# A retention layer's q and k of two heads as one seven-product block, three weight sums on GpSimd, and Newton's step with scalars

## The chip, the cores and the metric

The kernel runs on one core of a Trainium2 chip. The metric is the device time of one execution in microseconds (us), the median of several runs. One execution was also taken with the hardware profiler; all rows quoted come from such an execution. The engines are TensorE (PE; its weight loads are PEld), VectorE (DVE), ScalarE (ACT), GpSimd (POOL) and SyncE (SP, which here only issues transfers).

## The reference

A trunk of two layers over 512 tokens of 1024 channels, in float32. What matters here is the token half of a layer:

```python
proj = x @ w_in[i]
q_na, k_na, v_na, q_r, k_r, v_r, g_r, gate_a, gate_b = jnp.split(proj, IN_SPLITS, axis=-1)
ya = neighbourhood_attention(q_na, k_na, v_na, na_rpb[i])
yb = bidirectional_retention(q_r, k_r, v_r, g_r, ret_decay_f[i], ret_decay_b[i])
merged = sigmoid(gate_a) * (ya @ w_branch_a[i]) + sigmoid(gate_b) * (yb @ w_branch_b[i])
x = layer_norm(ALPHA * x + merged @ w_out[i], ln1_g[i], ln1_b[i])
ffn = conv_glu_ffn(x, w_up[i], conv_w[i], conv_b[i], w_down[i])
x = layer_norm(ALPHA * x + ffn + ple, ln2_g[i], ln2_b[i])
```

Retention has four heads; q_r and k_r have 128 channels per head, v_r and g_r 256. q_r and k_r are turned by a rotary embedding (cosine and sine of the position, the two halves of the 128 channels exchanged) and k_r is scaled by 128 ** -0.5. Each head then works in chunks of 128 tokens, forwards and backwards, with decays that are exponentials of learnt rates times distances.

## The kernel before

**Precision.** PE multiplies in a rounded form of float32. Every operand is therefore split into a high part (the rounded value, made by ACT) and a low part (the rest, a subtraction on DVE); `split` does this, and `mm3` issues three matmuls for one product: high by high, high by low, low by high.

**Weights.** All weights are packed as chunks of 128x1024 (512 KB), `wpack[l, c]`. A `Stream` holds the list of all chunks in the order of use. `load` issues transfers from SP into staging buffers (a ring of three, `raw`, or a buffer of the unit pool, `rawa` and `rawt` in the traces), `prep` splits a chunk into high and low parts (in a ring of three pairs, or in units where the chunk is "held"), and `get` hands it over and prepares some that follow.

**Blocks of seven products.** A projection can be cut into 2x2 blocks of inputs and outputs and done by seven block products instead of eight (Strassen's scheme in Winograd's form). The products are called `a`, `c`, `t1`, `t2`, `d`, `t3`, `t4`. The sums of weights that they need are made by transfers that add: `Stream.add` issues from POOL a transfer that reads a second chunk and adds it to the staging buffer. An `Item` is one chunk of this list; `plus` names the chunk to be added, `nxt` the item that takes over its staging buffer. The sums of the activations (`Sx`) are made once for each layer in `vg_sums`. Values and gates of retention are two such blocks (0 and 1, with outputs along the free dimension), and three blocks of gate columns (2, 3, 4) are done transposed by `gate_block` and `product_t`: 256 output columns by 512 tokens, in 24 matmuls of 128x256 for each product. Each block ends in `gate_out`, a sigmoid and a transfer to memory.

**Heads of q and k.** `q_head` and `k_head` do one head in a plain product: `gemm_t`, 24 matmuls of 128x512, then `rotated` (three multiplications by cosine and sine on DVE, an addition, a split). `q_head` also makes the head's decays (`decays`: two DVE operations and three exponentials on ACT) and a second q scaled by them (`qx`).

**Order.** After the values and gates of a layer comes the filling stretch. `FILL` is its list of pieces, written out by hand: products of blocks 2 to 4 (`2a` ... `4t4`), heads (`q0`, `k0`, ...), queries, keys and values of the attention (`nq`, `nk`, `vn`), and projections of the branches (`bb`). `RET_AT` and `NA_AT` say at which place of the list each head of retention and attention starts; its steps are put between the pieces. `ret_head` is a generator: scores and kz transposes first (`s`, `kz`), then the state (`st`), the output (`o`), the transposes (`ybt`). In this stretch a scheduler orders the instructions of each engine from the order of the program and the data; each engine then carries out its own list strictly in order, with semaphores between. In the other stretches the order is kept as written.

**The end.** The last layer norm of the last tile (tile 3) is done by `last_tile`: ACT's square root, then `refine` (a reciprocal and one step of Newton's method on values of one column), then two halves scaled and sent. Tile 2 is finished before by `norm_b`, whose last step is an addition on POOL and a transfer from SP.

Of the kernel before, what the change touches and what calls it, by code (L numbers as in the profile page):

```python
# [10 lines left out]
F32R = mybir.dt.float32r  # L11
# [4 lines left out]
P = 128  # L16
# [23 lines left out]
DEEP = 5  # L40

XN_AT = (0, 0, 0, 0)

FILL = ('2a', '3a', '2c', '3c', 'q0', '2t1', '3t1', 'k0', '2t2', '3t2', '2d', '3d', '4a', '2t3', '3t3', '4c', '2t4', '4t1', 'k1', '3t4', '4t2', '4d', 'q1', '4t3', '4t4', 'nk0', 'nq0', 'k2', 'q2', 'nk1', 'q3', 'nq3', 'k3', 'nq1', 'nk2', 'nq2', 'nk3', 'vn', 'bb0', 'bb1', 'bb2', 'bb4', 'bb5', 'bb6', 'bb7', 'xn', 'bb3')
# [22 lines left out]
VG_EARLY = "d"  # L67
VG_HELD = (('0t1', '1t1', '0t2', '0c', '1t2', '1a', '1d', '1t3'), ('0a', '0c', '0t1', '1t1', '1t3', '1t2', '0t3', '0t2', '1d'))

# [47 lines left out]
def trunk(tc, wpack, x_nat, x_tr, head, p_tr, rpb, decay, ln_par, ln_col, conv, cos_t, sin_t, dist, xi_d, zd, mask, ident_d, out):  # L117
# [4 lines left out]
    with ExitStack() as es:  # L122
# [50 lines left out]
        class Item:  # L173
# [7 lines left out]
            def __init__(self, kind, src, width, pool=None, plus=None, own=None):  # L181
                self.kind, self.src, self.width, self.pool, self.plus, self.own = kind, src, width, pool, plus, own
                self.raw = self.hl = None
                self.nxt = self.early = self.block = None
                self.sent = kind == "w" and any(a <= src[1] < b for a, b in SENT)

        def block_items(pos, held, early, n=2):
# [44 lines left out]
        def fill_items(l):  # L232
            by = {}

            for b in range(2, 5):
                pos = {(q, 0): (l, (36, 40, 56)[b - 2] + i, 0, 1024) for i, q in enumerate("acbd")}
                for it in block_items(pos, {}, VG_EARLY, 1):
                    by[f"{b}{it.kind}"] = [it]
# [36 lines left out]
        class Stream:  # L275
# [59 lines left out]
            def prep(self, n, part=None):  # L335
                while self.nprep < min(n, len(self.seq)):
# [317 lines left out]
        for l in range(DEPTH):  # L654
# [133 lines left out]
            def rotated(t1, ps, sc):  # L788
# [13 lines left out]
                return u  # L802

            def decays(h):

# [9 lines left out]

            kfs = {}

            def gate_a(m):
# [4 lines left out]
            def q_head(h):  # L823
                wx[h] = decays(h)
                t1 = tmp("t1")
                qr[h] = rotated(t1, gemm_t(xs), None)
                nc.vector.tensor_mul(t1, t1, wx[h][:, 1, :])
                u = qx[h] = unit_r("qx")
                split(u[:, 0, :], u[:, 1, :], t1)

            def k_head(h):
# [3 lines left out]
                kr[h] = rotated(kf[h], gemm_t(xs), P ** -0.5)  # L835


            def ret_head(h):
                q, k, k1, W = qr.pop(h), kr.pop(h), kf.pop(h), wx.pop(h)[:, 0, :]
                A = []  # L840
                for c in range(2):
# [3 lines left out]
                    for i in range(2):  # L845
                        m = slice((2 * c + 1 - i) * P, (2 * c + 2 - i) * P)
                        mm3(ps[:, i * 256:(i + 1) * 256], k[:, 0, m], k[:, 1, m], q[:, 0, n], q[:, 1, n], True, True)
                    ta = tmp("ta")
# [29 lines left out]
                for tq in range(2):  # L878
                    ps = bank("o")
                    for i in range(2):  # L880
# [7 lines left out]
                        d = slice((1 - tq) * 256, (2 - tq) * 256)  # L888
                        mm3(o, qq[:, 0, c], qq[:, 1, c], su[:, 0, d], su[:, 1, d], False, True)
                    st = sp.tile([P, 2, 6], F32, tag="bn", name=nm("gn"))  # L890
# [204 lines left out]
            def gate_block(b, kind):  # L1095
# [34 lines left out]
                else:  # L1130
                    assert (b, "p5") not in keep
                    product_t(kind, u[b], False)
                    t = tmp("sgb")
                    nc.scalar.activation(t, u[b], AF.Sigmoid)
# [31 lines left out]
            def fillers():  # L1166
                for i, f in enumerate(FILL):
# [3 lines left out]
                    if f == "xn":  # L1171
                        plain_x()
                        continue
                    if f[0] in "234":
                        gate_block(int(f[0]), f[1:])
# [242 lines left out]
            for s, n in enumerate(SEGS):  # L1418
# [254 lines left out]
def _pack(w_in, w_ba, w_bb, w_out, w_up, w_down, w_pg, w_pp):  # L1673
# [3 lines left out]
    for hp in range(2):  # L1677
        ch += list(vr[hp]) + list(gr[hp])
        for h in (2 * hp, 2 * hp + 1):
            ch += [qr[h], kr[h]]  # L1680
# [88 lines left out]
```

## Time and profile before

| | us |
|---|---|
| median of 3 runs | 1684.12 (1683.38 to 1684.5) |
| the profiled execution, its own time | 1682.4 |
| its span, first to last instruction | 1680.6 |

The granted clock of TensorE was 0.998 in this execution. A row of a group gives the line, the engine, the operation, out<-in with shapes, the number of instructions, their busy time and the mean duration of one in ns, and the idle time of the engine just before them. A row in order of time gives start and duration in us. A line number is often that of a helper; names of tiles tell more. "lo<-raw" is the DVE half of a split of weights, "hi<-raw" the ACT half.

### The profile page before, as it was taken

How to read it: one execution, taken by the hardware profiler on the slowest of the kernel's cores; microseconds unless marked ns; L12 is line 12 of the kernel's file. 1: busy time of each engine (PE TensorE's matmuls, PEld its weight loads, DVE VectorE, ACT ScalarE, POOL GpSimd, SP SyncE). 2: the span in 40 equal slices, each digit the busy share in tenths (PEclk: the TensorE clock that was granted, in tenths of full speed). 3: DMA queues.
4: the chain of work that ended last, by engine and by line, in shares of the span. 5: the costliest groups of instructions: out<-in, count | busy, mean ns of one | idle time of the engine just before them, and what ended most of it. 6: DMA issues, size and time to landing. Idle time of an engine off the chain costs nothing.

```text
span 1680.6 us, 22093 instructions
## 1 busy us (share of the span) xinstructions
PE 1668.9 (99%) x8327; PEld 1417.6 (84%) x8327; DVE 1229.6 (73%) x1860; ACT 951.7 (57%) x1420; POOL 187.8 (11%) x213
## 2 busy tenths in 40 slices
PE   9999999999999999999999999999999999999997
PEld 7889988888888888888888899888888888888886
DVE  7656677776788767767876567777698887676678
ACT  6764676863366545344476647768534574453454
POOL 1111111100200100000112011111002010000003
PEclk9999999999999999999999999999999999999999
DMA  8989666666655535535779796666667464264274
GB/s 305 251 229 240 166 147 138 170 168 233 200 131 168 121 113 160 139 103 177 200 225 220 183 246 158 139 141 168 169 242 236 129 167 121 88 198 115 89 213 100
DMA packets 87530, 290.20 MB, mean 173 GB/s; under 512 B 9984, under 2 KB 14592, under 8 KB 87424
## 3 DMA queue, kind: packets, MB, share of 16 engines
q1 hardware_dynamic: 62368, 199.66, 33.4%
q0 software_dynamic: 25056, 89.14, 29.7%
q8 instruction: 65, 1.06, 0.3%
q14 instruction: 41, 0.34, 0.1%
HBM read 269.89 MB, written 17.83 MB: 171 GB/s over the span
## 4 chain that ended last, share of the span: by engine, by line
PE 98%; DVE 1%; ACT 0%; issue 0%; DVEq 0%; ACTq 0%
PE gt L90 31%; PE u L90 13%; PE v L90 7%; PE gt L397 6%; PE gt L398 6%; PE gt L399 6%; PE w L90 4%; PE gn L398 3%; PE gn L399 3%; PE gn L397 3%; PE x L90 1%; PE u L397 1%; PE u L399 1%; PE u L398 1%; PE gn L90 1%; PE na L1023 1%
## 5 line engine op out<-in xcount | busy, mean ns | idle before, releaser
L90 PE MATMUL gt<-x1t,hi 128*128 128x512 f32 x1408 | 433.4, 389 | 0.0
L90 PEld LDWEIGHTS gt<-x1t,hi 128*128 128x128 f32 x1408 | 264.3, 188 | 54.6
L90 PE MATMUL gt<-x1t,lo 128*128 128x512 f32 x704 | 274.1, 389 | 0.1
L90 DVE TENSOR_TENSOR lo<-raw,hi 128x1024 fp32r<-128x1024 f32 (+1 forms) x147 | 176.0, 1207 | 44.1 <-ACT hi L90 44.0
L90 DVE SCALAR_TENSOR_TENSOR ca<-gt,cw,ca 128x511 f32<-128x511 f32 x176 | 131.8, 749 | 78.2 <-ACT ca L90 75.1
L90 ACT CAST hi<-raw 128x1024 fp32r<-128x1024 f32 (+1 forms) x147 | 151.3, 1039 | 34.2 <-PE u L90 15.1
L90 PEld LDWEIGHTS gt<-x1t,lo 128*128 128x128 f32 x704 | 132.1, 188 | 28.6 <-DVE lo L90 1.0
L90 DVE TENSOR_TENSOR lo<-rawa,hi 128x1024 fp32r<-128x1024 f32 x94 | 109.8, 1177 | 48.8 <-ACT hi L90 48.6
L90 ACT ACTIVATE ca<-gt,cw 128x512 f32<-128x512 f32 x88 | 68.7, 780 | 131.3 <-PE gt L90 131.3
L90 ACT CAST hi<-rawa 128x1024 fp32r<-128x1024 f32 x94 | 94.5, 1016 | 39.0 <-DMA rawa<-in_wpack 14.1
L90 POOL DMA_DIRECT2D rawa<-in_wpack x72 | 65.1, 949 | 367.9 <-DVE lo L90 315.1
L397 PE MATMUL gt<-xt,hi 128*128 128x512 f32 x256 | 100.8, 394 | 0.0
L398 PE MATMUL gt<-xt,hi 128*128 128x512 f32 x256 | 99.8, 390 | 0.0
L399 PE MATMUL gt<-xt,lo 128*128 128x512 f32 x256 | 99.7, 389 | 0.0
L170 ACT CAST hi<-raw 128x1024 fp32r<-128x1024 f32 x44 | 45.9, 1053 | 75.1 <-issue 29.6
L355 ACT CAST hi<-raw 128x1024 fp32r<-128x1024 f32 x48 | 50.5, 1053 | 48.8 <-PE gt L398 41.1
L357 POOL DMA_DIRECT2D lo<-in_wpack x48 | 42.2, 879 | 294.3 <-ACT lo L356 221.1
L90 POOL DMA_DIRECT2D rawt<-in_wpack x20 | 18.8, 1007 | 380.5 <-DMA rawt<-in_wpack 371.9
L171 DVE TENSOR_TENSOR lo<-raw,hi 128x1024 fp32r<-128x1024 f32 x44 | 53.4, 1224 | 10.7 <-ACT hi L170 10.2
L399 PEld LDWEIGHTS gt<-xt,lo 128*128 128x128 f32 x256 | 48.1, 188 | 10.3
L90 PE MATMUL v<-hi,sa 128*128 128x512 f32 x176 | 56.2, 389 | 0.0
L397 PEld LDWEIGHTS gt<-xt,hi 128*128 128x128 f32 x256 | 48.2, 188 | 9.1
(353 smaller groups left out, 4219.6 us busy)
## 6 DMA issues: line engine op xcount, KB each, us to landing
raw<-in_wpack SPq DMA_DIRECT2D x235, 512.0 KB, 3.6
rawa<-in_wpack POOLq DMA_DIRECT2D x84, 512.0 KB, 6.4
lo<-in_wpack POOLq DMA_DIRECT2D x48, 512.0 KB, 5.4
rawa<-in_wpack SPq DMA_DIRECT2D x28, 512.0 KB, 6.8
rawt<-in_wpack SPq DMA_DIRECT2D x28, 512.0 KB, 6.7
rawt<-in_wpack POOLq DMA_DIRECT2D x28, 512.0 KB, 7.6
r_scr<-pp SPq DMA_DIRECT2D x8, 512.0 KB, 10.1
gb<-gb_scr SPq DMA_DIRECT2D x8, 512.0 KB, 4.8
```

The source lines that it names most:

```text
L90: r = f(*a, **k)
L170: nc.scalar.copy(hi, src)
L171: nc.vector.tensor_sub(lo, src, _f(hi))
L355: nc.scalar.copy(hi[:, cs], it.raw[:, cs])
L357: nc.gpsimd.dma_start(lo[:, cs], wpack[l, c][:, o:o + w], accum_op=ALU.add)
L397: nc.tensor.matmul(ps, lh, rh, start=start, stop=False, skip_group_check=more)
L398: nc.tensor.matmul(ps, lh, rl, start=False, stop=False, skip_group_check=more)
L399: nc.tensor.matmul(ps, ll, rh, start=False, stop=stop, skip_group_check=more)
L1023: nc.tensor.matmul(ov[kt], lv, pt[kt // 2][:, sp_, c], start=i == 0 and sp_ == 0, stop=i == 3 and sp_ == 1)
```

## The change

Three edits, with the orders that belong to them.

1. q and k of retention heads 0 and 1 become block 5 of the filling stretch: a transposed block of seven products over the 256 columns of q and the 256 of k together. `gate_block` and `product_t` do it as they do blocks 2 to 4; in place of the sigmoid and the transfer, `qk_out` does rotary embedding, scaling and splits for one half of the tokens and q or k of both heads at a time. Q, QX and K then lie in two tiles for two halves of the tokens, and `ret_head` reads them through small functions (`whole`, `halves`). The four pieces `q0`, `k0`, `q1`, `k1` leave `FILL`, seven pieces `5a` to `5t4` enter it and the others are put in a new order; `RET_AT` and `NA_AT` are moved by three. The decays of both heads are made at the first half of q.
2. `POOLED`: for `t2` and `t3` of block 2 and `t2` of block 3 the chunk `d` is not added by a transfer, but by an addition on POOL from the staging buffer of item `d`, after that item has been split.
3. In `refine` the product of the variance with the reciprocal twice is a `tensor_scalar` with two per-partition scalars instead of a `scalar_tensor_tensor`.

In layer 0 product `t2` of block 1 is no longer held in units.

```diff
+POOLED = ('t2 t3', 't2', '', '')
...
-FILL = ('2a', '3a', '2c', '3c', 'q0', '2t1', '3t1', 'k0', '2t2', '3t2', '2d', '3d', '4a', '2t3', '3t3', '4c', '2t4', '4t1', 'k1', '3t4', '4t2', '4d', 'q1', '4t3', '4t4', 'nk0', 'nq0', 'k2', 'q2', 'nk1', ...)
-RET_AT = (21, 26, 30, 34)
-NA_AT = (36, 36, 39, 40, 42, 43, 43, 44)
+FILL = ('2a', '3a', '2c', '3c', '2t1', '3t1', '2d', '3d', '2t2', '3t2', '5a', '5c', '4a', '5t1', '2t3', '3t3', '2t4', '5t2', '5d', '3t4', '4c', '5t3', '4t1', '5t4', '4d', '4t2', '4t3', 'k2', '4t4', 'q2', 'nk0', 'nq0', 'nk1', ...)
+RET_AT = (24, 29, 33, 37)
+NA_AT = (39, 39, 42, 43, 45, 46, 46, 47)
...
-VG_HELD = (('0t1', '1t1', '0t2', '0c', '1t2', '1a', '1d', '1t3'), ...)
+VG_HELD = (('0t1', '1t1', '0t2', '0c', '1a', '1d', '1t3'), ...)
...
-                    it = Item(kind, at(src), pos["a", j][3], plus=at(plus), own=kind in ("a", "t3"), pool=held.get(kind))
+                    it = Item(kind, at(src), pos["a", j][3], plus=None if kind in pooled.split() else at(plus), own=kind in ("a", "t3"), pool=held.get(kind))
...
+            for it in out:
+                if it.kind in pooled.split():
+                    [o for o in out if o.kind == "d"][0].into.append(it)
...
-                        else:
+                        elif it.nxt.plus is not None:
                             self.add(it.nxt)
+                    for o in it.into:
+                        nc.gpsimd.tensor_add(o.raw, o.raw, it.raw)
...
+            def qk_out(fh, th, src):
+
+                v = lambda t: t.rearrange("p (h n) -> p h n", h=2)
+                n = slice(th * 256, (th + 1) * 256)
+                trig = lambda t, p: _ap(t[p], th * 256, [[0, 2], [1, 256]])
+                if fh == 0:
+                    t1 = v(tmp("t1"))
+                else:
+                    if 0 not in kfs:
+                        kfs[0] = unit_f("kf", (P, 2, 512))
+                    t1 = kfs[0][:, :, n]
+                t2 = tmp("t2")
+                lo, hi, al = slice(0, 64), slice(64, 128), slice(0, 128)
+                for o, i, tb in ((t1, al, cos_sb), (v(t2[hi]), lo, sin_sb), (v(t2[lo]), hi, sin_sb)):
+                    if fh == 0:
+                        nc.vector.tensor_mul(o, v(src[i]), trig(tb, i))
+                    else:
+                        nc.vector.scalar_tensor_tensor(o, v(src[i]), -P ** -0.5, trig(tb, i), op0=ALU.mult, op1=ALU.mult)
+                nc.vector.tensor_add(t1, t1, v(t2))
+                d = Qh if fh == 0 else Kh
+                u = d[th] = up.tile([P, 2, 2, 256], F32R, tag="u", name=nm("qk"))
+                split(u[:, 0], u[:, 1], t1)
+                if fh == 0:
+                    for h in range(2):
+                        if h not in wx:
+                            wx[h] = decays(h)
+                        nc.vector.tensor_mul(t1[:, h], t1[:, h], wx[h][:, 1, n])
+                    u = QXh[th] = up.tile([P, 2, 2, 256], F32R, tag="u", name=nm("qx"))
+                    split(u[:, 0], u[:, 1], t1)
...
             def gate_out(b, fh, th, src, scale=1.0):
+                if b == 5:
+                    qk_out(fh, th, src)
+                    return
                 nc.scalar.activation(src, src, AF.Sigmoid, scale=scale)
...
-                    nc.vector.scalar_tensor_tensor(a, r, ve[0], r, op0=ALU.mult, op1=ALU.mult)
+                    nc.vector.tensor_scalar(a, ve[0], r, r, op0=ALU.mult, op1=ALU.mult)
```

More of the change, by code (lines that the diff above doesn't have):

```diff
@@ L67 @@
 VG_EARLY = "d"
-VG_HELD = (('0t1', '1t1', '0t2', '0c', '1t2', '1a', '1d', '1t3'), ('0a', '0c', '0t1', '1t1', '1t3', '1t2', '0t3', '0t2', '1d'))
+VG_HELD = (('0t1', '1t1', '0t2', '0c', '1a', '1d', '1t3'), ('0a', '0c', '0t1', '1t1', '1t3', '1t2', '0t3', '0t2', '1d'))
 def _ap(t, off, dims):
@@ L184, in __init__, with block_items @@
                 self.nxt = self.early = self.block = None
+                self.into = []
                 self.sent = kind == "w" and any(a <= src[1] < b for a, b in SENT)
-        def block_items(pos, held, early, n=2):
+        def block_items(pos, held, early, n=2, pooled=""):
             out = []
@@ L233, in fill_items @@
             by = {}
-            for b in range(2, 5):
-                pos = {(q, 0): (l, (36, 40, 56)[b - 2] + i, 0, 1024) for i, q in enumerate("acbd")}
-                for it in block_items(pos, {}, VG_EARLY, 1):
+            for b in range(2, 6):
+                pos = {(q, 0): (l, (36, 40, 56, 8)[b - 2] + i, 0, 1024) for i, q in enumerate("acbd")}
+                for it in block_items(pos, {}, VG_EARLY, 1, POOLED[b - 2]):
                     by[f"{b}{it.kind}"] = [it]
@@ L802, in rotated @@
                 return u
+            kfs = {}
+            whole = lambda u: lambda s, c: u[:, s, c]
+            Qh, QXh, Kh = {}, {}, {}
+            halves = lambda u, h: lambda s, c: u[c.start // 256][:, s, h, c.start % 256:c.start % 256 + c.stop - c.start]
+            def qk_out(fh, th, src):
[26 more added lines that the diff above has]
+                    split(u[:, 0], u[:, 1], t1)
+                for h in range(2):
+                    if th in d and 1 - th in d:
+                        if fh:
+                            kr[h], kf[h] = halves(Kh, h), kfs[0][:, h]
+                        else:
+                            qr[h], qx[h] = halves(Qh, h), halves(QXh, h)
             def decays(h):
@@ L814, in decays @@
                 return w
-            kfs = {}
             def gate_a(m):
@@ L825, in q_head @@
                 t1 = tmp("t1")
-                qr[h] = rotated(t1, gemm_t(xs), None)
+                qr[h] = whole(rotated(t1, gemm_t(xs), None))
                 nc.vector.tensor_mul(t1, t1, wx[h][:, 1, :])
-                u = qx[h] = unit_r("qx")
+                u = unit_r("qx")
                 split(u[:, 0, :], u[:, 1, :], t1)
+                qx[h] = whole(u)
             def k_head(h):
@@ L834, in k_head @@
                 kf[h] = kfs[h // 2][:, h % 2, :]
-                kr[h] = rotated(kf[h], gemm_t(xs), P ** -0.5)
+                kr[h] = whole(rotated(kf[h], gemm_t(xs), P ** -0.5))
             def ret_head(h):
@@ L1132, in gate_block @@
                     product_t(kind, u[b], False)
+                    if b == 5:
+                        qk_out(0, 1, u[b])
+                        return
                     t = tmp("sgb")
@@ L1173, in fillers @@
                         continue
-                    if f[0] in "234":
+                    if f[0] in "2345":
                         gate_block(int(f[0]), f[1:])
@@ L1678, in _pack @@
         ch += list(vr[hp]) + list(gr[hp])
+        if hp == 0:
+            qk = np.concatenate([q_r[:, :256], k_r[:, :256]], axis=1)
+            ch += [qk.reshape(2, 4, P, 2, 256)[int(k in "cd"), :, :, int(k in "bd")].transpose(1, 0, 2).reshape(P, 1024) for k in "acbd"]
+            continue
         for h in (2 * hp, 2 * hp + 1):
```

6 lines of the change are left out of this document (3 added, 3 removed).

## The prediction

> **What bounds the kernel now.** I read the page first (span, busy time, chain that ended last), then who TensorE (PE) waited for, then PE in order of time where the change lies.
>
> ```profile
> span 1680.6 us, 22093 instructions
> PE 1668.9 (99%) x8327; PEld 1417.6 (84%) x8327; DVE 1229.6 (73%) x1860; ACT 951.7 (57%) x1420; POOL 187.8 (11%) x213
> ...
> PE 98%; DVE 1%; ACT 0%; issue 0%; DVEq 0%; ACTq 0%
> ```
>
> ```profile
> PE warm L504 <- DVE warm L501: 1.2, 1, 1.2
> ```
>
> PE is busy 99% of the span, the chain that ended last is PE for 98% of it, and in the whole run PE's only recorded wait is 1.2 us, before the warm-up. So between about 5 us and the last matmul the time is PE's own work: work taken from PE is gained in full, and any operand that comes late is paid in full. The other engines have room on average only (VectorE, DVE, 73%; ScalarE, ACT, 57%).
>
> ```profile
> 162.53 0.28 PE L397 MATMUL w<-xt,hi 128*128 128x256 f32 x1
> ...
> 165.41 0.28 PE L397 MATMUL u<-xt,hi 128*128 128x256 f32 x1
> ...
> 168.29 0.28 PE L397 MATMUL v<-sh,hi 128*128 128x256 f32 x1
> ...
> 171.17 0.40 PE L397 MATMUL gt<-xt,hi 128*128 128x512 f32 x1
> ...
> 176.64 0.28 PE L397 MATMUL u<-xt,hi 128*128 128x256 f32 x1
> ...
> 182.39 0.28 PE L397 MATMUL s<-qk,qk 128*128 128x256 f32 x1
> ...
> 184.19 0.36 PE L397 MATMUL v<-sh,hi 128*128 128x256 f32 x1
> ```
>
> These are the first matmuls of neighbouring pieces of the filling stretch. A block product (24 matmuls of 256 columns) takes 165.41 - 162.53 = 2.88 us, the next one again 2.88: 0.120 us a matmul. A plain head of q or k (24 of 512 columns) takes 176.64 - 171.17 = 5.47 us. The two score pieces and four transposes of a retention head take 184.19 - 182.39 = 1.80 us.
>
> **The change part by part.**
>
> *PE's work.* Per layer four plain heads (4 x 5.47 = 21.88) become seven products (7 x 2.88 = 20.16): 1.72 less, 3.4 us in two layers. Nothing else on PE changes in number. As PE waits for nothing, this is gained if no operand comes late. So the question is what comes late.
>
> *What stands beside it.* Per layer the block needs seven splits instead of four (ACT cast and DVE subtraction), three copies of PSUM and three additions more. Averages leave room; queues decide. The rows for that:
>
> ```profile
> L171 DVE TENSOR_TENSOR lo<-raw,hi 128x1024 fp32r<-128x1024 f32 x44 | 53.4, 1224 | 10.7 <-ACT hi L170 10.2 <-PE u L399 0.2
> ...
> L849 DVE TENSOR_TENSOR ta<-s,wx 128x512 f32<-128x512 f32 x16 | 11.1, 692 | 15.0 <-PE s L399 14.8
> ...
> L791 DVE TENSOR_TENSOR t<-gt,cos_sb 128x512 f32<-128x512 f32 x8 | 5.5, 690 | 11.1 <-PE gt L399 11.1
> ...
> L799 DVE TENSOR_TENSOR t<-t,t 128x512 f32<-128x512 f32 x8 | 5.5, 690 | 0.2
> ...
> L1105 DVE TENSOR_TENSOR p<-p,w 128x512 f32<-128x512 f32 x6 | 4.1, 688 | 4.0 <-PE w L399 4.0
> ```
>
> ```profile
> L170 ACT CAST hi<-raw 128x1024 fp32r<-128x1024 f32 x44 | 45.9, 1053 | 75.1 <-issue 29.6 <-PE gt L398 29.0 <-PE u L398 7.7
> ...
> L170 ACT CAST a<-ta 128x512 fp32r<-128x512 f32 x16 | 9.6, 621 | 4.6 <-DVE ta L849 4.4
> ...
> L812 ACT ACT_TABLE_LOAD x6 | 7.7, 1283 | 0.1
> ...
> L170 ACT CAST qk<-t 128x512 fp32r<-128x512 f32 x8 | 5.0, 623 | 3.8 <-DVE t L799 3.8
> L170 ACT CAST qx<-t 128x512 fp32r<-128x512 f32 x8 | 5.0, 620 | 6.0 <-DVE t L827 6.0
> ...
> L861 ACT ACTIVATE kz<-kz,zeta 128x128 fp32r<-128x128 f32 x32 | 11.6, 364 | 4.2 <-DVE kz L862 4.1
> ...
> L811 ACT ACTIVATE wx<-wx 128x384 f32<-128x384 f32 x8 | 4.2, 522 | 0.0
> ...
> L812 ACT ACTIVATE wx<-xi_sb,lgs 128x256 f32<-128x256 f32 x8 | 4.1, 508 | 0.1
> ...
> L813 ACT ACTIVATE wx<-xi_sb,lgs 128x256 f32<-128x256 f32 x8 | 4.0, 499 | 0.0
> ...
> L1111 ACT COPY p<-v 128x512 f32<-128x512 f32 x6 | 3.5, 579 | 0.0
> ```
>
> ```profile
> 177.55 0.68 DVE L797 SCALAR_TENSOR_TENSOR t<-gt,sin_sb 64x512 f32<-64x512 f32 x1
> 178.25 0.69 DVE L798 SCALAR_TENSOR_TENSOR t<-gt,sin_sb 64x512 f32<-64x512 f32 x1
> 178.97 1.23 DVE L171 TENSOR_TENSOR lo<-raw,hi 128x1024 fp32r<-128x1024 f32 x1
> 180.11 0.68 DVE L799 TENSOR_TENSOR kf<-kf,t 128x512 f32<-128x512 f32 x1
> ```
>
> The last rows tell how such rows add up: rotary halves start 0.70 and 0.72 apart (no overlap), other neighbours start some 0.09 before the former's end (178.97 + 1.23 against 180.11).
>
> *First late operand: the weights of `2t4`.* In the changed program's order, product `5c` is followed on DVE by the addition of p1 and w, the three rotary multiplications of q's first half, a split that belongs to `2t3`, and the rotary addition; then on ACT by the cast of Q, a table load, six exponentials (the decays of both heads), the cast of QX, a copy of `5t1`, and only then the cast of `2t4`'s weights; DVE then makes their low part. By rows: 0.69 + 3 x 0.70 + 1.22 + 0.69 = 4.70; 0.62 + 1.28 + 2 x 0.51 + 2 x 0.50 + 2 x 0.52 + 0.62 + 0.58 + 1.05 = 7.21; and 1.22: 13.1 us, some 12.2 with the overlaps. It starts 0.16 us after PE goes on (a 256-column matmul lasts 0.28 and its follower starts after 0.12). PE's cover is four products (`4a`, `5t1`, `2t3`, `3t3`) and two matmuls, 4 x 2.88 + 0.24 = 11.76. Late by 0.6; bounds 0.3 (everything overlaps) and 1.5 (nothing does). With some hand-overs between engines I take 0.8. In the kernel before, the decays stood in two heads apart, each with a 5.47 us head beside it.
>
> *Second: retention head 0.* Its first step now stands directly behind `5t4`, which completes q. Chain: DVE three rotary multiplications, the score scaling of the first piece, the rotary addition (3 x 0.70 + 0.69 + 0.69 = 3.48), ACT's cast of Q 0.62, DVE's low part 0.69, the rest of the second score piece with its end 5 x 0.12 + 0.16 = 0.76, scaling 0.69, and on ACT the cast 0.62 before the first quarter of kz that `st` needs, 0.36: 3.48 + 0.62 + 0.69 + 0.76 + 0.69 + 0.62 + 0.36 and the 0.16 at the start make 7.4. In front of Q's cast ACT has a whole split (up to 1.05), and in front of the second piece's cast those of QX and of the first piece (up to 1.24). PE's cover is 1.80 + `4d` + `4t2`, 7.56. Late between 0 and 2.1; I take 1.2, a little over the middle since the order does put those casts there. It shows partly at the second score piece, partly at `st`.
>
> So 2.0 us a layer, 4.0 in two (bounds 0.6 to 7.2), against 3.4 gained.
>
> *Sums by GpSimd (POOL) and the transfers.* The block has four plain and four accumulating loads where the heads had four plain ones; three accumulations (`t2`, `t3` of block 2, `t2` of block 3) become POOL additions: one transfer more a layer, SP's loads unchanged in number.
>
> ```profile
> rawt<-in_wpack POOLq DMA_DIRECT2D x28, 512.0 KB, 7.6
> ```
>
> ```profile
> 140.00:150.00 10.00, 10.00 (x76) 9.57 (x75) 6.31 (x8) 4.65 (x6) 2.27 (x3) 1.00 1.05 234
> 150.00:160.00 10.00, 10.00 (x85) 10.00 (x85) 5.67 (x7) 4.81 (x7) 0.86 (x1) 1.00 1.04 302
> ```
>
> Without them it would be four more where the DMA engines are already full (1.05 and 1.04) and an accumulation lands 7.6 us after its issue; with them I take the transfers as before, cost 0. The lower bound is 0 too, since PE waits for no transfer now; the upper is rival C. On POOL's queue an addition that waits for its operands holds the accumulations behind it, and on SP's the next load into the staging buffer that an addition still reads waits for POOL, with the loads behind it: at most 2.34 us (below) each, taken at 0 as loads run some products ahead.
>
> ```profile
> 1672.36 2.34 POOL L90 TENSOR_TENSOR R<-R,lnb 128x1024 f32<-128x1024 f32 x1 [1.26 <-ACT R L90]
> ...
> 1673.27 1.45 DVE L90 SCALAR_TENSOR_TENSOR ra<-ri,ve 128x1 f32<-128x1 f32 x1
> ...
> 1674.72 2.41 SPq L90 DMA_DIRECT2D out<-R  x3
> ```
>
> A POOL addition of 128x1024 takes 2.34 us. In the same rows stands what it does to DVE: Newton's step of one column, two SBUF tensors in, takes 1.45 us and ends as the addition ends (1674.72 and 1674.70). So a DVE operation with two SBUF inputs waits for a running POOL addition. [...] The splits stand ahead, though: the low part that started at 178.97 was ready at 180.20 and is used by the product that starts at 184.19, a lead of 4 us against 2.34. I take 0 and keep it as a rival.
>
> *Newton's step with scalars.* The step stays one instruction but has one tensor input and two per-partition scalars.
>
> ```profile
> L995 DVE TENSOR_SCALAR nmx<-nmx 128x4 f32<-128x4 f32 x16 | 2.6, 165 | 0.0
> ```
>
> By this row it takes 0.17, so DVE ends 1.28 us sooner. But the outputs bound that:
>
> ```profile
> DMA  6999799989999999669999999400000000000000
> GB/s 117 211 187 281 140 257 187 211 164 281 351 375 398 375 445 468 258 258 375 398 363 410 375 386 375 187 23 23 12 0 0 0 0 0 0 0 0 0 0 0
> ```
>
> (40 slices of 1674 to 1681 us.) The 512 KB of tile 2 are issued when POOL's addition ends (1674.72, unchanged), the two halves of tile 3 queue behind them, and from about 1675.6 to 1678.5 the engines are nine tenths busy in all slices but three. The halves coming sooner finds them full. Between 0 and 1.28; I take 0.3, near the end that the busy row shows.
>
> *The held `t2` of block 1* (layer 0) goes to the ring of three pairs: 0, at most one split late once (1.05 + 1.22 = 2.3).
>
> Sum: -3.4 + 4.0 - 0.3 = +0.3 us. The profiled execution took 1682.4 us (span 1680.6), so 1682.7 by its own count; the median of the runs shown is 1684.12, 1.7 above it, hence 1684.4. What a measurement of this kernel can tell is about 0.2%, 3.4 us: the forecast is no measurable change.
>
> **The rivals.** *A, nothing comes late.* PE's only wait of 1.2 us speaks for it: the order may give these chains more overlap than I count. Then -3.4 - 0.3, at best -4.7 with the whole Newton step: 1680.4 (1679.4). Against it: both chains are longer by rows than their cover.
>
> [...] The POOL additions hold DVE in the stretch where the splits are made. It decides where a split's lead is under 2.34 us, as after the value stage when block 2 begins; one of three additions exposed in each layer gives 2 x 2.34 = 4.7 on top: 1689.1. All six would give 14. For it: the 1.45 us; against it: the 4 us lead.
>
> *C, transfers late.* The DMA engines are full over 140 to 160 us now, and in the change 27 short products (2.88) follow each other where four heads of 5.47 lay between. If one accumulated load a layer comes 2 us late: +4, 1688.4. Against it: three accumulations less.
>
> *D, it does not do what it says*: the Newton step alone; already in the sum.
>
> **How the numbers follow.** Forecast 0.64, A 0.16, B 0.10, C 0.10. The forecast's own range is 1682 to 1687 (0.8 to 3.3 us late a layer); to hold 8 in 10 it reaches most of the way to A and to C: 1680.8 to 1688.2. Faster by over 0.2% (under 1680.7) is most of A and a little of the forecast's low bound: 0.16. Slower by over 0.2% (over 1687.5) is B and most of C: 0.17. The rest, 0.67, is within.
>
> **What would show it.** Right: PE's product rows 2.88 us apart with block 5 among them, its matmul records up by 144, and gaps of about 0.8 before the second weights of `2t4` and about 1.2 together before head 0's second score piece and `st`, alike in both layers; in the tail the step at about 0.2 us and the outputs ending at the same distance from the last matmul, within half a microsecond. Wrong: no gaps there (A); DVE subtractions of more than 2 us beside POOL additions with PE idle behind them (B); PE waiting behind ACT casts that wait for a landing (C).

## The result

The changed kernel takes 1685.28 us (median of 22 runs, 1683.46 to 1687.93), the kernel before 1683.34 (22 runs, 1681.95 to 1684.7): a ratio of 1.0014, 95% interval 1.0008 to 1.002. That is slower by a little, within the 0.2% called no change. The profiled execution took 1686.13 us, its span 1684.4. On its page the span, PE's busy time and the chain that ended last answer to the rows of before:

```profile
span 1684.4 us, 22425 instructions
PE 1667.5 (99%) x8471; PEld 1422.4 (84%) x8471; DVE 1246.6 (74%) x1876; ACT 950.3 (56%) x1426; POOL 203.3 (12%) x221
...
PE 95%; DVE 2%; ACT 1%; issue 1%; DMA 0%; DVEq 0%; ACTq 0%
```

PE has 8471 - 8327 = 144 more matmuls and is busy 1.4 us less, yet the end is later: PE now waits. Whom it waited for in the whole run (total us, times, longest):

```profile
PE u L408 <- DVE lo L173: 1.5, 2, 0.8
PE st L406 <- ACT kz L910: 1.4, 2, 0.7
PE warm L513 <- DVE warm L510: 1.2, 1, 1.2
PE s L406 <- ACT qk L172: 0.8, 2, 0.6
PE s L407 <- DVE qk L173: 0.3, 1, 0.3
```

Before, only the warm-up's line stood here. The others are the two late operands of the prediction: the low part of `2t4`'s weights, and head 0's scores and states. They make 4.0 us in two layers.

**Where the time went.** PE's order of time gives two landmarks in each layer: the first matmul of block 2 and the first of the up projection. In layer 1 of the changed kernel:

```profile
108.61 0.28 PE L406 MATMUL u<-xt,hi 128*128 128x256 f32 x1
...
453.50 0.47 PE L92 MATMUL u<-hi,x1t 128*128 128x512 f32 x1
```

Before, the same two are these:

```profile
108.72 0.28 PE L397 MATMUL u<-xt,hi 128*128 128x256 f32 x1
...
452.43 0.48 PE L90 MATMUL u<-hi,x1t 128*128 128x512 f32 x1
```

So this stage took 343.71 and takes 344.89 us; in layer 2 343.69 and 344.94. The two stages together are 2.43 us longer. Everything between and behind them is unchanged: 490.46 and 490.54 us from the up projection to the next layer's block 2, 383.29 and 383.39 from the second up projection to the last matmul's start. What is left of the span's 3.8 us lies at the end: the last instruction ends 10.76 us after that matmul's start before, 12.00 after.

The table has the same readings for every kernel profiled here. The start and the end vary by a microsecond and more from one execution to the next even where nothing of them was changed; the rest between the stages is 490.4 to 490.6 and 383.3 to 383.4 in all. So the stages tell what an edit did to PE in one execution, and the ratio of timed runs what it did in all.

| kernel | block 2 starts | stage, layer 1 | layer 2 | sum | end after the last matmul's start | ratio to before (95%) |
|---|---|---|---|---|---|---|
| before | 108.72 | 343.71 | 343.69 | 687.40 | 10.76 | 1 |
| before, again (e11) | 108.51 | 343.67 | 343.67 | 687.34 | 10.48 | 1.0001 (0.9992 to 1.001) |
| Newton's step alone (e4) | 109.35 | 343.71 | 343.78 | 687.49 | 11.80 | 1.0002 (0.9993 to 1.001) |
| changed kernel | 108.61 | 344.89 | 344.94 | 689.83 | 12.00 | 1.0014 (1.0008 to 1.002) |
| `1t2` held (e8) | 109.49 | 344.16 | 345.70 | 689.86 | 10.57 | 1.001 (1.0001 to 1.0019) |
| four POOL sums (e7) | 109.33 | 344.19 | 345.16 | 689.35 | 10.51 | 1.001 (1.0001 to 1.0019) |
| no POOL sums (e6) | 109.36 | 346.64 | 344.63 | 691.27 | 10.65 | 1.0035 (1.0021 to 1.0049) |
| decays early (e1) | 109.06 | 343.76 | 345.15 | 688.91 | 10.54 | 1.0008 (0.9999 to 1.0017) |
| head 0 later (e2) | 109.55 | 343.13 | 343.81 | 686.94 | 10.68 | 1.0005 (0.9996 to 1.0013) |
| e1 and e2 together (e3) | 109.22 | 343.18 | 343.83 | 687.01 | 10.61 | 1.0004 (0.9995 to 1.0013) |
| e3, two POOL sums (e5) | 108.63 | 343.77 | 342.58 | 686.35 | 12.22 | 1.0005 (0.9996 to 1.0014) |
| the same again (e10) | 109.18 | 345.95 | 343.63 | 689.58 | 10.72 | 1.001 (1.0 to 1.0019) |
| e5, old Newton step (e9) | 109.43 | 345.90 | 342.78 | 688.68 | 10.78 | 1.0004 (0.9995 to 1.0012) |

**The first wait.** PE, DVE and ACT around `2t4` in the changed kernel, in order of time:

```profile
160.28 0.28 PE L407 MATMUL u<-xt,hi 128*128 128x256 f32 x1
161.32 0.39 PE L408 MATMUL u<-xt,lo 128*128 128x256 f32 x1 [0.76 <-DVE lo L173]
161.54 0.28 PE L406 MATMUL u<-xt,hi 128*128 128x256 f32 x1
```

```profile
148.88 0.69 DVE L1157 TENSOR_TENSOR p<-p,w 128x512 f32<-128x512 f32 x1 [0.71 <-PE w L408]
...
160.04 1.23 DVE L173 TENSOR_TENSOR lo<-rawa,hi 128x1024 fp32r<-128x1024 f32 x1 [0.74 <-ACT hi L172]
```

```profile
153.59 0.62 ACT L172 CAST qk<-t 128x512 fp32r<-128x512 f32 x1 [0.43 <-DVE t L836]
154.23 1.28 ACT L862 ACT_TABLE_LOAD   x1
...
158.96 1.05 ACT L172 CAST hi<-rawa 128x1024 fp32r<-128x1024 f32 x1
```

The chain stands there in the forecast's order: from the addition of p1 and w (148.88) over Q's cast, the table load, the exponentials, QX's cast and the copy to the weights' low part, ready at 160.04 + 1.23 = 161.27. That is 12.39 us; the forecast had 12.2 to 13.1.

**The second wait**, at head 0 behind `5t4`:

```profile
189.38 0.28 PE L407 MATMUL u<-sl,hi 128*128 128x256 f32 x1
189.87 0.39 PE L406 MATMUL s<-qk,qk 128*128 128x256 f32 x1 [0.21 <-ACT qk L172]
190.10 0.60 PE L905 MATMUL kz<-ident,kf 128*128 128x128 f32 x4
190.96 0.39 PE L407 MATMUL s<-qk,qk 128*128 128x256 f32 x1 [0.26 <-DVE qk L173]
...
192.74 0.28 PE L408 MATMUL u<-sh,lo 128*128 128x256 f32 x1
193.72 0.38 PE L406 MATMUL st<-vh,kz 128*128 128x256 f32 x1 [0.69 <-ACT kz L910]
```

Recorded waits: 0.21 + 0.26 + 0.69 = 1.16 us here, 0.56 + 0.71 = 1.27 in layer 2.

**What a wait costs.** The row at 161.32 says that PE waited 0.76 us. But between neighbours that do not wait starts are 0.12 apart, and here they are 161.32 - 160.28 = 1.04; the next start follows after 0.22 instead of 0.12. So PE lost 0.92 + 0.10 = 1.02 us: a recorded wait begins at the end of a matmul whose follower would have started 0.16 us earlier, and the first matmul after it holds its own follower up by 0.10. The 0.16 is the difference between a matmul's 0.28 us (an end that the profile models) and the 0.12 from its start to the next. At head 0 the same count over all these starts gives 1.99 us in layer 1 and 2.04 in layer 2. Together 2 x 1.02 + 1.99 + 2.04 = 6.1 us, against 4.0 of recorded waits.

**The POOL sums.** POOL's second and third addition in layer 1 of the changed kernel, and DVE's splits beside them:

```profile
122.30 2.40 POOL L376 TENSOR_TENSOR rawa<-rawa,raw 128x1024 f32<-128x1024 f32 x1 [3.15 <-DVE lo L173]
126.64 2.40 POOL L376 TENSOR_TENSOR rawa<-rawa,raw 128x1024 f32<-128x1024 f32 x1 [1.94 <-DVE p L1157]
```

```profile
123.87 1.91 DVE L173 TENSOR_TENSOR lo<-rawa,hi 128x1024 fp32r<-128x1024 f32 x1 [0.28 <-ACT hi L172]
...
126.79 4.47 DVE L173 TENSOR_TENSOR lo<-raw,hi 128x1024 fp32r<-128x1024 f32 x2 [0.32 <-ACT hi L172]
```

Each addition holds a split: the one of 123.87 ends at 125.78, 1.08 us after the addition (122.30 + 2.40 = 124.70), about a split's time of 1.23; and the pair of 4.47 us would take some 2.4. So POOL's additions do hold DVE, which is rival B; but PE waits for none of these splits.

**The end** of the changed kernel:

```profile
1674.84 2.35 POOL L92 TENSOR_TENSOR R<-R,lnb 128x1024 f32<-128x1024 f32 x1 [1.26 <-ACT R L92]
...
1675.75 0.27 DVE L92 TENSOR_SCALAR ra<-ve,ri 128x1 f32<-128x1 f32 x1
...
1677.21 1.59 SPq L92 DMA_DIRECT2D out<-R  x3
```

Newton's step takes 0.27 us in the midst of POOL's addition, so it is not held. DVE ends 5.7 us after the last matmul's start instead of 6.9. The end does not follow.

Each row's stages come from one execution. The one changed version that was profiled twice, e5 and e10, has sums 3.2 us apart, so a difference of two sums alone settles little; gaps that come again at the same place settle more. The profiled executions of e2, e3 and e5 also lie 1.1 to 1.4 us under the medians of their runs, that of the changed kernel 0.85 above its own. By the medians, each against its own runs of the kernel before, e1, e2 and e3 are only 1.2 to 1.4 us faster than the changed kernel, and their intervals overlap its interval. So what follows on single waits is read from the traces; no timed run sets e1, e2 or e3 apart from the changed kernel.

### The profile page after: what moved, and what is told of

It reads as the page before. It is cut to its first block, busy times and chain, and to the rows that moved or that the text cites. A ratio compares the mean times of both kernels' runs of the same rounds, so it can differ in the third digit from the quotient of the medians.

```text
span 1684.4 us, 22425 instructions
## 1 busy us (share of the span) xinstructions
PE 1667.5 (99%) x8471; PEld 1422.4 (84%) x8471; DVE 1246.6 (74%) x1876; ACT 950.3 (56%) x1426; POOL 203.3 (12%) x221
## 3 DMA queue, kind: packets, MB, share of 16 engines
q8 instruction: 66, 1.08, 0.3%
## 4 chain that ended last, share of the span: by engine, by line
PE 95%; DVE 2%; ACT 1%; issue 1%; DMA 0%; DVEq 0%; ACTq 0%
PE gt L92 31%; PE u L92 13%; PE v L92 7%; PE gt L406 5%; PE gt L408 5%; PE gt L407 5%; PE w L92 4%; PE gn L408 3%; PE gn L406 3%; PE gn L407 3%; PE x L92 1%; PE gn L92 1%; PE u L408 1%; PE u L407 1%; PE u L406 1%; PE na L1072 1%
## 5 line engine op out<-in xcount | busy, mean ns | idle before, releaser
L92 DVE TENSOR_TENSOR lo<-rawa,hi 128x1024 fp32r<-128x1024 f32 x94 | 109.6, 1176 | 50.2 <-ACT hi L92 50.0
L92 ACT CAST hi<-rawa 128x1024 fp32r<-128x1024 f32 x94 | 94.1, 1014 | 38.7 <-DMA rawa<-in_wpack 14.7
L362 ACT CAST hi<-raw 128x1024 fp32r<-128x1024 f32 x48 | 50.4, 1050 | 63.5 <-PE gt L407 59.0
L406 PE MATMUL gt<-xt,hi 128*128 128x512 f32 x192 | 75.8, 395 | 0.0
L172 ACT CAST hi<-raw 128x1024 fp32r<-128x1024 f32 x40 | 41.6, 1050 | 60.1 <-PE gt L407 27.3
L407 PE MATMUL gt<-xt,hi 128*128 128x512 f32 x192 | 74.9, 390 | 0.0
L408 PE MATMUL gt<-xt,lo 128*128 128x512 f32 x192 | 74.9, 390 | 0.0
L173 DVE TENSOR_TENSOR lo<-rawa,hi 128x1024 fp32r<-128x1024 f32 x32 | 40.5, 1266 | 25.6 <-ACT hi L172 25.6
L172 ACT CAST hi<-rawa 128x1024 fp32r<-128x1024 f32 x32 | 33.5, 1048 | 40.4 <-DMA rawa<-in_wpack 17.4
```

The source lines that it names most:

```text
L92: r = f(*a, **k)
L172: nc.scalar.copy(hi, src)
L173: nc.vector.tensor_sub(lo, src, _f(hi))
L362: nc.scalar.copy(hi[:, cs], it.raw[:, cs])
L406: nc.tensor.matmul(ps, lh, rh, start=start, stop=False, skip_group_check=more)
L407: nc.tensor.matmul(ps, lh, rl, start=False, stop=False, skip_group_check=more)
```

## The experiments

**e1: the decays ahead of `5a`.**

```diff
 # fillers(), ahead of gate_block
+if f == "5a":
+    for h in range(2):
+        wx[h] = decays(h)
```

> The changed kernel, but the decays of heads 0 and 1 (a table load and six exponentials on ScalarE) are issued two products earlier, ahead of `5a`, instead of between the casts of Q and QX. Theory (first term of the forecast: this work stands in ScalarE's queue ahead of the cast of `2t4`'s weights): the gap before the second weights of `2t4` (1.04 us from start to start against a usual 0.12, and 0.10 more behind it, in both layers) goes, 1.0 us a layer, so 2.0 us less than the changed kernel: about 1683.3, level with the kernel before. The gaps at head 0 stay. Rival (another split in front of it is as late, or the table load only moves the wait to an earlier product): the gap stays or moves, 0 to 0.5 us less than the changed kernel.

Measured: the stages are 0.92 us shorter than in the changed kernel, not 2.0. The gap at `2t4` is gone in both layers, and a new one is there in both, 0.52 + 0.10 us at `2d`. DVE, POOL and PE of this kernel:

```profile
122.57 2.89 DVE L859 TENSOR_SCALAR wx<-dist_sb,nlg 128x384 f32<-128x384 f32 x2
...
129.35 4.48 DVE L173 TENSOR_TENSOR lo<-raw,hi 128x1024 fp32r<-128x1024 f32 x2 [0.43 <-ACT hi L172]
```

```profile
122.74 2.50 POOL L376 TENSOR_TENSOR rawa<-rawa,raw 128x1024 f32<-128x1024 f32 x1 [3.36 <-DVE lo L173]
129.00 2.40 POOL L376 TENSOR_TENSOR rawa<-rawa,raw 128x1024 f32<-128x1024 f32 x1 [3.76 <-DVE lo L173]
```

```profile
131.90 0.28 PE L407 MATMUL v<-sl,hi 128*128 128x256 f32 x1
132.54 0.39 PE L408 MATMUL v<-sh,lo 128*128 128x256 f32 x1 [0.36 <-DVE lo L173]
```

The scheduler took the decays far ahead, to 122.6 us, beside a POOL addition. Their two first operations took 2.89 us together; in the changed kernel the same pair takes 0.74:

```profile
155.21 0.74 DVE L859 TENSOR_SCALAR wx<-dist_sb,nlg 128x384 f32<-128x384 f32 x2
```

What follows on DVE is later, the third addition starts at 129.00 instead of 126.64, and the first split beside it, held like those above, ends at 132.49, where PE waits for it until 132.54. So the theory of the first wait holds, and the gain was partly given back to POOL's additions (rival B). The timed median is 1683.90 us, where about 1683.3 was expected.

**e2: head 0 two pieces later.**

```diff
-RET_AT = (24, 29, 33, 37)
+RET_AT = (26, 30, 33, 37)
```

> The changed kernel, but the steps of retention head 0 start two pieces of the filling stretch later, and those of head 1 one piece later, so that two products (`4d`, `4t2`) stand between `5t4` and the scores. Theory (second term: the rotary embedding and the splits of q's second half have 1.80 + 5.76 us of cover and need more): the gaps before the second score piece, before its later matmuls and before `st` (0.37 + 0.45 + 0.85 us and some 0.1 behind each) go, 1.6 to 2.0 us a layer, 3.2 to 4.0 in all: about 1681.5. The gap before `2t4`'s second weights stays. Rival (the chain of scaling and kz casts inside the head is too long by itself, wherever it stands): the gap before `st` stays, at most 1.7 us less than the changed kernel.

Measured: 2.89 us less in the stages; the timed median is 1683.77 us, where about 1681.5 was expected. PE's waits of this kernel:

```profile
PE u L408 <- DVE lo L173: 1.5, 2, 0.8
PE warm L513 <- DVE warm L510: 1.2, 1, 1.2
PE u L406 <- ACT u L1170: 0.6, 1, 0.6
```

All waits at `s` and `st` are gone, so the chain was long only for its place; `2t4`'s stay. The 0.6 us (0.80 + 0.10 from start to start, layer 2 alone) is new; without it the stages would be 3.8 us shorter, within the 3.2 to 4.0 expected. Here a product waits for its bank of PSUM, which ACT copies late.

**e3: both.** The two edits above together.

> Both of these edits at once: the decays ahead of `5a`, head 0 two pieces and head 1 one piece later. Theory (the two waits are independent, and with them the change would bring what PE's arithmetic promises, 3.4 us): 5.2 to 6.0 us less than the changed kernel, about 1679.5, and 3 to 4 less than the kernel before; PE without a gap of over 0.3 us between the warm-up and the end. Rival (the waits are fed by a shared cause, ScalarE or VectorE being full over the stretch, and come back elsewhere): less than 4 us under the changed kernel.

Measured: 2.82 us less than the changed kernel in the stages, not 5.2 to 6.0; the timed median is 1683.73 us, not 1679.5. `2t4` waits no more, but e1's gap of 0.62 is there in both layers, 0.5 us at a score in layer 1, and 1.15 us in layer 2 at a product that waits for a copy on ACT. The rival is right for half of the gain: the waits come back elsewhere.

**e4: Newton's step alone**, on the kernel before.

```diff
-nc.vector.scalar_tensor_tensor(a, r, ve[0], r, op0=ALU.mult, op1=ALU.mult)
+nc.vector.tensor_scalar(a, ve[0], r, r, op0=ALU.mult, op1=ALU.mult)
```

> The kernel before, with Newton's step by two per-partition scalars as the only edit. All theories: the step takes about 0.27 us instead of 1.45, and VectorE's last operation ends 1.2 us sooner after the last matmul. Theory (the output transfers bind): the time falls by 0 to 0.5 us (0.3 taken). Rival 1 (the chain of VectorE binds): 1.2 us less. Rival 2 (the halves of the last tile, issued sooner, only crowd the transfers already under way): 0 to 1 us more.

Measured: 1683.58 us against 1683.14, ratio 1.0002 (0.9993 to 1.001). A gain of 1.2 us, to 0.9993, is at the very edge of this interval; DVE ended 5.72 us after the last matmul's start, and the profiled end lay at 11.8. The step gains nothing that shows.

**e5: both edits, and two POOL sums instead of three.**

```diff
-POOLED = ('t2 t3', 't2', '', '')
+POOLED = ('t2 t3', '', '', '')
```

> The version with both waits removed (decays ahead of `5a`, head 0 two pieces and head 1 one piece later), and POOLED = ('t2 t3', '', '', ''): the sum of `3t2` is made by an accumulating transfer again, so there are two POOL additions a layer instead of three. Theory (in that version the decays' first VectorE operations stand beside the POOL addition for `3t2` at 122.9 us and one of them took 2.55 us instead of 0.41, which made the low part for the product at 131.9 us late: 0.52 and 0.10 us in both layers): these gaps go, 1.2 us less in all than that version, and the time from the first product of block 2 to the up projection falls from 343.2 and 343.8 to about 342.6 and 343.2. Rival 1 (the decays make VectorE and ScalarE late by their number alone): the gaps stay. Rival 2 (the transfer for `3t2` comes late in the full stretch): a gap of 1 us or more at `3t2`.

Measured: the gap at 132 us is gone from both layers, but not in the way that was expected. DVE and POOL of this kernel:

```profile
122.15 2.90 DVE L859 TENSOR_SCALAR wx<-dist_sb,nlg 128x384 f32<-128x384 f32 x2
...
128.93 1.23 DVE L173 TENSOR_TENSOR lo<-raw,hi 128x1024 fp32r<-128x1024 f32 x1 [0.43 <-ACT hi L172]
```

```profile
122.32 2.50 POOL L376 TENSOR_TENSOR rawa<-rawa,raw 128x1024 f32<-128x1024 f32 x1 [2.90 <-DVE lo L173]
```

The addition beside the decays is still there and holds them as before. The one that went, the sum for `3t2`, is the third, which in e1 stood at 129.00 beside the split for `2d`; that split takes 1.23 us now and is ready at 130.16. So the gap needs the third addition, as rival B has it. How much of it the held decays add, by making that split late, was not tested alone. Layer 2 takes 342.58 us, 1.11 less than the kernel before, the shortest stage seen here. The timed median, 1684.25 us, is no lower than that of the kernel before (1683.19). Layer 1 lost 1.79 + 0.10 us at `4t3`, which e10 explains.

**e6: no POOL sums.** POOLED = ('', '', '', '') in the changed kernel.

> The changed kernel without POOL additions, POOLED = ('', '', '', ''): all sums of weights by accumulating transfers. Theory (the DMA engines are full where blocks 2 and 3 run, and the additions relieve them without holding PE): PE waits for low parts whose transfer landed late, between 125 and 170 us and the same in the second layer, 2 to 5 us a layer, so 4 to 10 us more than the changed kernel. [...]

Measured: the stages are 1.44 us longer in the profiled execution, which is the fastest of four (1686.84 to 1690.13, median 1689.62); the ratio is 1.0035 (1.0021 to 1.0049) against 1.0014 (1.0008 to 1.002). This stretch of e6, and the same of the changed kernel (us, then PE, PEld, DVE, ACT and POOL, clock, DMA share, GB/s), and the ACT row that held PE in e6:

```profile
130.00:140.00 10.00, 8.79 (x73) 8.59 (x73) 3.39 (x3) 4.06 (x6) 0.86 (x1) 1.00 1.05 304
```

```profile
130.00:140.00 10.00, 10.00 (x86) 10.00 (x85) 4.93 (x5) 3.75 (x5) 1.96 (x3) 1.00 0.75 175
```

```profile
134.75 1.05 ACT L172 CAST hi<-rawa 128x1024 fp32r<-128x1024 f32 x1 [3.89 <-DMA rawa<-in_wpack]
```

With the sums as transfers the DMA engines are full (1.05 against 0.75) and a cast waits 3.89 us for a landing, with PE behind it. So the POOL sums pay: 1.4 us by the profile, some 0.2% or 3.5 us by the ratios, where 4 to 10 were expected. In the profile the loss stands in layer 1 alone.

**e7: four POOL sums.** POOLED = ('t2 t3', 't2 t3', '', '').

> The changed kernel with one more POOL addition a layer, POOLED = ('t2 t3', 't2 t3', '', ''): `t3` of block 3 too. Theory (splits lead their products by more than the 2.4 us for which an addition holds VectorE): the time from the first product of block 2 to the up projection stays at 344.9 us in both layers within 0.3, though one more split of VectorE is stretched to about 2 us or more. [...]

Measured: 344.19 and 345.16 us, 0.5 less in sum, and no new gap of PE. Layer 1 is 0.7 us shorter, more than the 0.3 asked; layer 2 is within it. In layer 1 the waits at the score pieces are missing; those at `2t4` and `st` are there. POOL of this kernel, and the split on DVE in front of the first of these additions:

```profile
125.37 3.40 POOL L376 TENSOR_TENSOR rawt<-rawt,raw 128x1024 f32<-128x1024 f32 x1
128.73 3.39 POOL L376 TENSOR_TENSOR rawa<-rawa,raw 128x1024 f32<-128x1024 f32 x1
```

```profile
124.59 1.91 DVE L173 TENSOR_TENSOR lo<-rawa,hi 128x1024 fp32r<-128x1024 f32 x1 [0.28 <-ACT hi L172]
```

These two additions take 3.4 us instead of 2.4: a split that came first holds the addition too. The one above runs until 126.50, 1.13 us into the addition of 125.37. All of it stays hidden. So the three additions of the changed kernel are not yet too many.

**e8: `1t2` held again** in layer 0 of the program, which is layer 1 of the table.

```diff
-VG_HELD = (('0t1', '1t1', '0t2', '0c', '1a', '1d', '1t3'), ...)
+VG_HELD = (('0t1', '1t1', '0t2', '0c', '1t2', '1a', '1d', '1t3'), ...)
```

> The changed kernel with product `t2` of block 1 in layer 0 held in units again, as in the kernel before. Theory (the cost of this edit is 0): the first stage, up to the first product of block 2, and the time from there to the up projection stay as in the changed kernel within 0.3 us. Rival: a split late once, so 0.5 to 2.3 us less than the changed kernel in layer 0 alone.

Measured: 344.16 + 345.70 = 689.86, against 689.83. The sum is the same, but its parts are not within the 0.3 asked: block 2 starts 0.9 us later (109.49), layer 1 takes 0.7 less, and layer 2, in which the edit changes nothing, 0.8 more. So a layer differs by up to 0.8 us from execution to execution now; layer 1's 0.7 less is no proof of the rival, as e7 shows the same without this edit. A cost of `1t2` is not seen, but one of less than a microsecond could not be.

**e9 and e10: the version of e5 with the old Newton step, and once more as it was.**

> The version with both waits removed and two POOL additions a layer, with Newton's step as in the kernel before (scalar_tensor_tensor). What is open is whether the new step brings or costs anything at the end. Theory (output transfers bind, the step is worth 0 to 0.5 us): the step is held by the POOL addition again (about 1.45 us), VectorE ends 6.9 instead of 5.7 us after the last matmul starts, and the outputs end in the same interval of 10.5 to 12.2 us after it; the time is that of the same version with the new step, within 0.5 us. Rival 1 (crowding: the halves of the last tile, sent sooner, now and then hold the transfer of tile 2): the end lies at about 10.8 us and the median is 0.5 to 1 us lower. Rival 2 (VectorE's chain binds): 1.2 us more.

> The version with both waits removed and two POOL additions a layer once more, for the comparison with the old step on the same chip, and to see whether the gap of 1.79 us that its first layer showed before a product of block 4 (a cast that waited for an accumulated load, issued 7.3 us before) comes again. Theory (a landing that varies): the gap is there or not, in either layer, and the two layers take between 341.9 and 343.8 us from block 2 to the up projection, where the kernel before takes 343.7 in both. Rival (a fixed lateness of that load): the same gap in layer 1 again and none in layer 2.

Measured: 1684.16 us with the old step, 1684.77 with the new; the ratios 1.0004 and 1.001 have overlapping intervals. With the old step DVE ended 6.89 us after the last matmul's start and the outputs at 10.78. In e10, with the new step, they were 5.72 and 10.72. This speaks against rival 2, by which the ends would lie 1.2 us apart, and leaves rival 1 open by the times alone. The gap at `4t3` was there again in layer 1 of both, 1.93 us from start to start in e9 and 2.12 in e10, and in layer 2 of neither; ACT, POOL and PE of e10:

```profile
193.41 1.04 ACT L172 CAST hi<-rawa 128x1024 fp32r<-128x1024 f32 x1 [2.43 <-DMA rawa<-in_wpack]
194.36 0.58 ACT L1170 COPY u<-u 128x512 f32<-128x512 f32 x1
```

```profile
185.79 0.86 POOL L312 DMA_DIRECT2D rawa<-in_wpack  x1 [4.83 <-DVE lo L173]
```

```profile
194.99 0.39 PE L406 MATMUL u<-sh,hi 128*128 128x256 f32 x1 [1.93 <-ACT u L1170]
```

An accumulated load issued at 185.79 lands at about 193.4; the cast of these weights waits for it at the head of ACT's queue, and behind it stands the copy that frees PE's bank. So the rival is right: the lateness belongs to the place. That part of the expectation about 341.9 to 343.8 us failed as well; layer 1 took 345.9 in both, since two more gaps, of 0.3 to 1.0 us between 152 and 157 us, came on top. They have the form of late transfers too: the cast in front of the first waited 3.27 us (e9) and 2.77 us (e10) for a landing, in e5 1.04. Why e5's transfer was not late I can't show.

**e11: the kernel before, unchanged.**

> The kernel before, unchanged, for a second profile of its start and its end: how far these vary from one execution to the next. Expected by the runs so far: the first product of block 2 starts between 108.6 and 109.6 us, the two stages from there to the up projection take 343.7 us each within 0.1, and the outputs end 10.5 to 12.2 us after the start of the last matmul; by the crowding theory always at about 10.8.

Measured: the stages as expected; the start of block 2 (108.51) and the end (10.48) both lie just under the ranges given, so the end varies by 0.3 us in this kernel too. The kernel before keeps its stages to 0.04 us; the changed versions, which have no slack left, do not.

No version is faster than the kernel before: all ratios are 1.0001 or more.

## Why the prediction was right, and where a term was off

*PE's work, -3.4.* Right, and 0.2 too much. At the usual distances from start to start (0.120, 0.227 and 0.109 us for 256, 512 and 128 columns) the matmuls of a stage make 342.83 us in the kernel before and 341.20 in every version with the new block: 1.63 us less a layer, 3.26 in two, where the forecast had 1.72 and 3.44. In e5's second layer, with the fewest gaps, 1.11 of it shows: 1.38 us are lost there against 0.86 before.

*`2t4`, 0.8 a layer.* Right in place and cause: 0.76 recorded in both layers, and again in e2, e6, e7 and e8. e1 proved the cause, since without the decays in that queue the gap is gone.

*Head 0, 1.2 a layer.* Right in place and cause: 1.16 and 1.27 recorded, partly at the second score piece, partly at `st`, and e2 proved that it is the place. "Alike in both layers" holds for `st` only (0.69 and 0.71). The score's part changes from layer to layer and from execution to execution: 0.47 and 0.56 here, nothing in layer 1 of e7 and e8.

*Their sum, +4.0.* This is the mis-sized term. That the recorded waits add up to the same 4.0 is chance. The forecast's lateness is the delay of a matmul's start (it adds the 0.16 us by which a matmul outlasts its follower's start), so starts are what it has to be compared with: 0.92 us a layer at `2t4` for its 0.8, about 1.7 at head 0 for its 1.2, 5.2 in all for 4.0. And behind each late start the next one comes 0.10 later than usual, eight times in two layers, for which the forecast had nothing. Together that is the 6.1. With it -3.4 + 6.1 = +2.7, near the +2.43 of the stages; with 4.0 the forecast had +0.6 for the same stages. (Counted over all starts, with the small delays that both kernels have, the losses rose from 1.74 to 7.43 us, and -3.26 + 5.69 is the +2.43.)

*The total, +0.3.* Measured is +1.9 us (1685.28 against 1683.34; 1.3 to 3.4 by the interval). What is missing, 1.6, has the sign of the 1.8 that the stages lack, and nearly its size. That the forecast's 1684.4 lies within 0.9 of 1685.28 is in part luck: it was built on the median of three runs, 1684.12, and 22 runs of the kernel before have 1683.34. The forecast of no measurable change held, but by the interval the kernel is a little slower.

*POOL sums and transfers, 0.* Right for this kernel: splits were held, and their lead covered it. A fourth sum brought no new gap (e7), and without sums it is slower (e6). Rival B came true as soon as other work was moved beside the additions (e1 and e3, 0.62 us a layer), rival C as soon as sums became transfers again (e5, e6, e10).

*Newton's step, -0.3.* Right in that the transfers bind. The chain was cut by 1.2 us and no timed run shows a gain: the last half of tile 3 is issued 6.91 us after the last matmul's start in e9 and 5.76 in e10, and lands at 9.51 and 9.44. The forecast that the end keeps its distance within 0.5 us failed in the profiled execution (12.00 against 10.76). In ten profiles with the new step the end lies seven times at 10.5 to 10.7 us and three times at 11.8 to 12.2; in three with the old step at 10.5 to 10.8. In the three late ones the transfers that POOL had issued for the earlier tiles end 7.7 to 8.1 us after the last matmul's start instead of 5.9 to 6.5, and in e4 three packets of theirs, started 3.6 to 3.7 us after that start, took 1.0 to 2.2 us instead of the usual 0.33. The halves of tile 3 are issued only from 5.3 us on, so at least there the sooner halves are not the cause; whether they ever are stays open.

*`1t2`, 0.* Not contradicted: e8 shows no cost, within the microsecond by which its parts vary.

*Rival A* fell at once by the waits.

## What to carry to other kernels

On an engine that is busy 99% of the time, size a late operand from start to start: the wait that the profile records is a lower bound, here short by about 0.26 us at each place. An arithmetic saving of 0.2% was lost in the queues of engines that were busy 56% and 74% on average, because the order put a table load and six exponentials before one cast that PE needed, and a head directly behind the product that completes its q. And in a stretch without slack a removed wait uncovers the next one, be it the hold of a POOL addition (0.62 us a layer in e1), a landing (1.93 at `4t3` in e9) or a bank (0.90 in e2): test such edits together, not only one by one.

## What was not expected of the hardware

DVE's first operation of the decays has one SBUF tensor in (128x384) and a scalar. It takes 0.41 us alone (0.411 to 0.415 in all eight of the changed kernel). Of the two in e1 the first, started before the POOL addition of 2.50, took 0.41, and the second 2.56, until 0.2 us after the addition's end; the forecast had only operations with two SBUF tensors held. Newton's step in the same form, but with one column, was not held: 0.27 us, inside an addition from 1674.84 to 1677.19. What makes the difference between the two, no run here shows.

The holding goes both ways: in e7 POOL's additions took 3.4 instead of 2.4 us where a split had come before them. By what way the two engines hold each other the traces do not tell.
